# One decoder block on one core: the second feed-forward's seven-product pair over all of K at chunks 7 and 8, and the attention branch in blocks of 512 columns

## The chip, the cores and the metric

The kernel runs on one core of a Trainium2 chip. The metric is the device time of one execution in microseconds. The core's engines run side by side and each takes its instructions in the order in which they are written down for it: TensorE (PE, matrix products into eight accumulator banks of 128 x 512 fp32), VectorE (DVE), ScalarE (ACT), GpSimd (POOL) and SyncE (SP), which issues the DMA transfers here.

## What is computed

One layer on 256 tokens of width 1024 in fp32: a SwiGLU feed-forward of hidden width 2816 at half weight, a mixing layer (attention and gated spatial mixing, merged by gates), a second feed-forward, and a last norm.

```python
def swiglu(x, w_gate, w_up, w_down):
    return (jax.nn.silu(x @ w_gate) * (x @ w_up)) @ w_down
...
h = h + 0.5 * swiglu(rmsnorm(h, ffn1_norm[l]), ffn1_w_gate[l], ffn1_w_up[l], ffn1_w_down[l])
n = rmsnorm(h, mix_norm[l])
...
y_attn = attn @ w_branch_attn[l]
y_gmlp = gm @ w_branch_gmlp[l]
gates = jax.nn.sigmoid(n @ w_gate[l] + b_gate[l])
merged = gates[..., :D] * y_attn + gates[..., D:] * y_gmlp
h = h + merged @ w_out[l]
h = h + 0.5 * swiglu(rmsnorm(h, ffn2_norm[l]), ffn2_w_gate[l], ffn2_w_up[l], ffn2_w_down[l])
return rmsnorm(h, final_norm)
```

## The kernel before

**Products in three matmuls.** Weights come from memory in fp32 and are split into a high part (a cast, on ScalarE) and a low part (a subtraction, on VectorE), in `split` (L255 to L258). A product of two split blocks takes three matmuls: high by high, high by low, low by high (`mm3`, L249 to L253). In the text a product is one such group of three for 128 tokens, 128 rows of K and up to 512 columns.

**Weight units.** All weights stand in one list, `units`, in the order in which TensorE wants them. A unit is a tile w0, w1, ...; it is loaded in two halves of 512 KB (raw, seven buffers), split half by half, and kept in a ring of five tiles (w). `unit(i, ahead)` splits up to `ahead` units past the one that is wanted, so VectorE and ScalarE work some units in front of TensorE.

**Chunks.** A feed-forward's gate and up matrices are cut into 11 chunks (`NC`) of 256 hidden features, each 512 columns: gate, then up. A plain chunk is two units (K in two halves) and 16 products into two banks, one for each half of the tokens (f2_90 and f2_91 are those of chunk 9 of the second feed-forward). Behind a chunk, `Hidden.glu` (L578) makes silu of the gate half on ScalarE (f2s), multiplies it by the up half on VectorE (f2a, two operations) and transposes it (f2t); DMAs carry it to another layout, and it is settled as a split operand (f2h).

**The pair of chunks.** `chunk_pair` (L408) computes two chunks together. `seven` (L378) takes two blocks of K and forms the 2 x 2 by 2 x 2 block product (token halves by chunks) in seven products in place of eight. It needs four combinations of the activations ("forms", made by `make_forms`, L399, on VectorE and split), and four combinations of the weights, which are made on VectorE as well: a "single" unit holds three quarters of the weights as they are, and the "sums" unit after it has four 512-wide additions (L205 to L208) and is then split like any other. Four of the products (p1, p5, p6, p7) go to banks shared by several outputs, the others to the banks acc0_0, acc0_512 and acc1_0. In both feed-forwards the pair is chunks 6 and 7, with `PAIR_K` = 3 sevens for the first six of K's eight blocks, and a rest unit with eight plain products for the last two. A copy of p1 on ScalarE (L421) and additions on VectorE (L422 to L425, L435) combine the banks. In the second feed-forward the units are w78 to w83 (single and sums by turns), w84 (the rest) and w85 for the start of chunk 8.

**Who sets the order.** In the first part of the first feed-forward the order on VectorE and ScalarE is the one written. In the second feed-forward a scheduler places the instructions of each engine when the program is built, and they run in that order. Buffers (the ring, the raws, the banks) are handed on by semaphores: a new user waits for the last reader.

**The merge.** `merge` (L1007) does one half of 512 columns of the two branches at a time; the spatial branch (pg) is 512 columns wide, the attention branch (pa) 256, for each quarter p and each token half j. VectorE multiplies by the gate, adds and transposes (L1023 to L1025), SP writes the quarter to memory (`m_way`) and reads it back in another layout (`from_way`); `settle` splits it into mg, the operand of the output product.

Of the kernel before, what the change touches and what calls it, by code (L numbers as in the profile page):

```python
# [46 lines left out]
PAIR = {"f1": 6, "f2": 6}  # L47
PAIR_K = 3
# [3 lines left out]
def block_kernel(ctx, tc, t, out):  # L52
# [63 lines left out]
    def add_chunks(name):  # L116


        c = PAIR[name]
        first = add_units(name, 2 * c)  # L120
        units.extend((f"{name}s2", i, what) for i in range(PAIR_K) for what in ("single", "sums"))
        units.extend((name, i) for i in range(2 * c, 2 * NC - 3))
        return first
# [173 lines left out]
    def token_factors(name):  # L297
# [15 lines left out]
        return [r[:, j:j + 1] for j in range(NT)]  # L313
# [64 lines left out]
    def seven(name, at, i, tokens_of, acc, shared, forms, last, ahead=DEEP):  # L378
# [18 lines left out]
        product(acc, name, (1, 0), d, of(w, 3), False)  # L397
# [10 lines left out]
    def chunk_pair(name, at, nT, forms, ahead):  # L408
# [7 lines left out]
        for i in range(PAIR_K):  # L416
            seven(name, at + 2 * i, i, tokens_of, acc, shared, forms[i], i == PAIR_K - 1, ahead)
# [9 lines left out]
        def rest(e):  # L427
            w = unit(at + 2 * PAIR_K, ahead)
            for k in range(2):
                for j in range(NT):  # L430
                    product(acc, name, (j, 512 * e), tokens_of(KB - 2 + k, j),
                            tuple(w[:, 2 * e + k, two, :] for two in range(2)), k == 1)
# [8 lines left out]
    def chunk_of(name, first, nT, c, forms):  # L441

        at = c - PAIR[name]
        if at == 0:
            pending[name] = chunk_pair(name + "p", first + 2 * c, nT, forms, DEEP)
        if at in (0, 1):
            return pending[name](at)
        return chunk(first + 3 * (at > 0), nT, name, c, ahead=DEEP)

    def pair_forms(name, tags, block):  # L450

        normed = []
        for n, rows in ((0, 4), (1, 2)):
            normed.append(sump.tile([P, 4, S // 32, 32], F32, tag="sum", name=f"{name}normed{n}"))
            for k in range(rows):
                block(4 * n + k, normed[n][:, k])

        def make():
            to = [act.tile([P, 2 - n, 4, 2, P], F32R, tag=tag, name=f"{name}forms{n}") for n, tag in enumerate(tags)]
            to = [to[0][:, 0], to[0][:, 1], to[1][:, 0]]  # L460
            for i in range(PAIR_K):
                make_forms(lambda j, k: normed[i // 2][:, 2 * (i % 2) + k, 4 * j:4 * j + 4, :], to[i], f"{name}form{i}")
            return to
        return make
# [102 lines left out]
    class Hidden:  # L567
# [10 lines left out]
        def glu(self, c, ps, rs):  # L578
            self.turned[c] = tmp.tile([P, NT, CH], F32, tag="hg", name=f"{self.name}t{c}")
            a = tmp.tile([P, NT, CH], F32, tag="a", name=f"{self.name}a{c}", bufs=1)  # L580
            for j in range(NT):
                sg = tmp.tile([P, CH], F32, tag="s", name=f"{self.name}s{c}{j}")
                nc.scalar.activation(sg, ps[j][:, :CH], AF.Silu, scale=rs[j])  # L583
                nc.vector.scalar_tensor_tensor(a[:, j], ps[j][:, CH:], rs[j], sg, op0=ALU.mult, op1=ALU.mult)
# [102 lines left out]
    with in_order():  # L687
        x = inputs_of(front[:, KB:KB + KB * ROW])
        split_to(f1 + 3)
# [5 lines left out]
        forms_of = pair_forms("f1p", ("nC", "ws"), lambda k, to: nc.scalar.activation(  # L695
            to.rearrange("p q c -> p (q c)"), x[:, k], AF.Identity, scale=front[:, k:k + 1]))
        sum_parts("1")
        sums.append(chunk(f1, nT, "f1", 1))
        rs = token_factors("1")
        sums.append(chunk(f1, nT, "f1", 2))  # L700
# [504 lines left out]
```

## Time and profile before

| what | value |
| --- | --- |
| time, median of 3 runs | 514.98 us (514.45 to 516.18) |
| profiled execution | 514.82 us, of which its span 513.1 us |
| TensorE's granted clock | 1.00 |
| DMA | 126.82 MB, mean 247 GB/s |
| GpSimd busy | 12.0 us |
| ScalarE busy | 299.8 us |

The rows of the profile give a start, a duration, the engine, the line of the kernel and the operation, with out<-in by the program's names. x2 in a row of the timeline stands for two instructions one behind the other, and its duration is for both. Durations of rows that follow each other overlap a little, since an instruction starts before its predecessor has quite ended; what an instruction costs its engine is the distance from its start to the next one's. A bracket at a row's end is idle time of the engine ahead of it, and what ended that.

### The profile page before, as it was taken

The page shows a single profiled execution, that of the slowest core. Times are in us where ns is not written, and L with a number is a line of the kernel's source. Part 1 is how long each engine was busy: PE and PEld are TensorE (multiplying, and loading weights), DVE is VectorE, ACT ScalarE, POOL GpSimd, SP SyncE. Part 2 cuts the span into 40 slices and gives each one's busy share as a digit, 9 for nine tenths or more (in the row PEclk, how much of TensorE's full clock was granted, in tenths as well). Part 3 has the DMA queues.
Part 4 walks back from the last instruction along what each step waited for, and adds up shares of the span by engine and source line. Part 5 has one row for each costly group of instructions (what it writes and reads, how often), then busy time and mean ns, then how long its engine had stood idle before and what let it go on. Part 6 is the DMA issues. An engine that isn't in the chain of part 4 may idle for free.

```text
span 513.1 us, 6849 instructions
## 1 busy us (share of the span) xinstructions
PE 505.6 (99%) x2359; PEld 421.3 (82%) x2359; DVE 442.9 (86%) x645; ACT 299.8 (58%) x427; POOL 12.0 (2%) x25
## 2 busy tenths in 40 slices
PE   8999999999999999999999999999999999999995
PEld 6888888888888888888888898888888888888884
DVE  6897999999997956589976776997979999999964
ACT  7984549546573736667465603767725756566702
POOL 0010000000000010000000000001000000000002
PEclk9999999999999999999999999999999999999999
DMA  8998587798765886796899664928799558999302
GB/s 316 374 327 335 138 294 255 256 310 278 232 211 201 282 310 206 194 335 240 205 375 309 247 192 142 319 91 270 249 275 295 203 160 259 349 351 283 136 0 82
DMA packets 63922, 126.82 MB, mean 247 GB/s; under 512 B 11664, under 2 KB 36752, under 8 KB 63760
## 3 DMA queue, kind: packets, MB, share of 16 engines
q1 hardware_dynamic: 63600, 126.06, 74.6%
q8 instruction: 18, 0.29, 0.2%
q10 hardware_dynamic: 288, 0.33, 0.2%
q14 instruction: 16, 0.13, 0.1%
HBM read 113.26 MB, written 13.11 MB: 246 GB/s over the span
## 4 chain that ended last, share of the span: by engine, by line
PE 97%; DMA 1%; DVE 0%; issue 0%; ACT 0%; POOLq 0%; DVEq 0%; POOL 0%; ACTq 0%
PE f L253 12%; PE f L252 12%; PE f L251 12%; PE accdown L253 4%; PE accdown L251 4%; PE accdown L252 4%; PE acch L253 4%; PE acch L252 4%; PE acch L251 4%; PE acc L225 3%; PE g L252 3%; PE g L253 3%; PE g L251 3%; PE acc L230 1%; PE accf2p L253 1%; PE accf2p L252 1%
## 5 line engine op out<-in xcount | busy, mean ns | idle before, releaser
L258 DVE TENSOR_TENSOR w<-raw,w 128x1024 fp32r<-128x1024 f32 (+1 forms) x180 | 204.0, 1173 | 15.7 <-ACT w L256 15.6
L256 ACT CAST w<-raw 128x1024 fp32r<-128x1024 f32 (+1 forms) x180 | 173.8, 1015 | 24.4 <-PE f L253 7.9
L253 PE MATMUL f<-w,n 128*128 128x512 f32 x272 | 105.8, 389 | 0.0
L251 PE MATMUL f<-w,n 128*128 128x512 f32 x272 | 105.8, 389 | 0.0
L252 PE MATMUL f<-w,n 128*128 128x512 f32 x272 | 105.8, 389 | 0.0
L252 PEld LDWEIGHTS f<-w,n 128*128 128x128 f32 x272 | 51.1, 188 | 10.6
L251 PEld LDWEIGHTS f<-w,n 128*128 128x128 f32 x272 | 51.1, 188 | 10.6
L253 PEld LDWEIGHTS f<-w,n 128*128 128x128 f32 x272 | 51.1, 188 | 10.6
L256 ACT CAST w<-sum 128x1024 fp32r<-128x1024 f32 x28 | 29.5, 1053 | 31.7 <-DVE sum L206 21.5
L258 DVE TENSOR_TENSOR w<-sum,w 128x1024 fp32r<-128x1024 f32 x28 | 33.8, 1218 | 0.5 <-ACT w L256 0.5
L251 PE MATMUL accdown<-w,f1h 128*128 128x512 f32 x68 | 26.5, 389 | 0.0
L252 PE MATMUL accdown<-w,f1h 128*128 128x512 f32 x68 | 26.5, 389 | 0.0
L253 PE MATMUL accdown<-w,f1h 128*128 128x512 f32 x68 | 26.5, 389 | 0.0
L251 PE MATMUL g<-w,n 128*128 128x512 f32 x64 | 24.9, 389 | 0.0
L252 PE MATMUL g<-w,n 128*128 128x512 f32 x64 | 24.9, 389 | 0.0
L251 PE MATMUL acch<-w,f2h 128*128 128x512 f32 x64 | 24.9, 389 | 0.0
L252 PE MATMUL acch<-w,f2h 128*128 128x512 f32 x64 | 24.9, 389 | 0.0
L253 PE MATMUL acch<-w,f2h 128*128 128x512 f32 x64 | 24.9, 389 | 0.0
L253 PE MATMUL g<-w,n 128*128 128x512 f32 x64 | 24.9, 389 | 0.0
L225 PE MATMUL acc<-mg,w 128*128 128x512 f32 x64 | 17.0, 393 | 0.0
L583 ACT ACTIVATE f2s<-f,rstd 128x256 f32<-128x256 f32 x18 | 8.1, 473 | 12.5 <-PE f L253 11.4
L256 ACT CAST mg<-mixed 128x256 fp32r<-128x256 f32 x8 | 2.9, 404 | 21.3 <-DMA mixed<-mway 21.3
(279 smaller groups left out, 918.5 us busy)
## 6 DMA issues: line engine op xcount, KB each, us to landing
raw<-in_f SPq DMA_DIRECT2D x72, 512.0 KB, 6.2
raw<-in_f2d SPq DMA_DIRECT2D x22, 512.0 KB, 7.4
raw<-in_gate SPq DMA_DIRECT2D x16, 512.0 KB, 6.3
raw<-in_f1s SPq DMA_DIRECT2D x14, 512.0 KB, 6.6
raw<-in_f1d SPq DMA_DIRECT2D x14, 512.0 KB, 5.2
raw<-in_out SPq DMA_DIRECT2D x8, 512.0 KB, 5.4
raw<-in_f2s SPq DMA_DIRECT2D x6, 512.0 KB, 6.9
f1way<-f1t SPq DMA_DIRECT2D x11, 256.0 KB, 6.5
```

What stands on the lines that cost most here:

```text
L225: nc.tensor.matmul(ps, st, both.rearrange("p two n -> p (two n)"), start=first, stop=last)
L230: nc.tensor.matmul(ps[:, n:], st, both[:, 0, :], start=False, stop=False)
L251: nc.tensor.matmul(ps, sh, mh, start=first, stop=False)
L252: nc.tensor.matmul(ps, sh, ml, start=False, stop=False)
L253: nc.tensor.matmul(ps, sl, mh, start=False, stop=last)
L256: nc.scalar.copy(hi, src)
L258: nc.vector.tensor_sub(lo, src, hi.bitcast(F32))
L583: nc.scalar.activation(sg, ps[j][:, :CH], AF.Silu, scale=rs[j])
```

## The change

1. A table `PAIRS` takes the place of `PAIR` and `PAIR_K`: the first feed-forward keeps chunks 6 and 7 with three sevens, the second has chunks 7 and 8 with four sevens over all of K, hence no rest unit. Its units are now w80 to w87, and w88 starts chunk 9.
2. With four sevens nothing is left for the fourth bank (acc1_512), so the last quarter comes out with its sign turned. It is handed on so, and `glu` multiplies it by the negated norm factor, which `token_factors` now makes as well (one small operation on VectorE behind GpSimd's power).
3. The forms of the second feed-forward's pair are made at chunk 4 for chunk 3, and in other buffers; the reloads of the residual (`ht1`, `ht`) and of the last gain move to other chunks.
4. The attention branch is computed 512 columns at a time. Its product, addition and transpose are 512 wide, one for each token half, and each half of the tokens is written out for both quarters at once, with eight smaller writes in place of four.

```diff
-PAIR = {"f1": 6, "f2": 6}
-PAIR_K = 3
+PAIRS = {"f1": {6: 3}, "f2": {7: 4}}
...
+        minus = small.tile([P, NT], F32, tag="minus", name=f"minus{name}", bufs=1)
+        nc.vector.tensor_scalar(minus, r, -1.0, None, op0=ALU.mult)
...
+        ends = last and whole
         w = unit(at, ahead)
         product(shared, name, (1,), a, of(w, 0), last)
-        product(acc, name, (0, 0), b, of(w, 1), False)
-        product(acc, name, (0, 512), form(3), of(w, 2), False)
+        product(acc, name, (0, 0), b, of(w, 1), ends)
+        product(acc, name, (0, 512), form(3), of(w, 2), ends)
...
-        for i in range(PAIR_K):
-            seven(name, at + 2 * i, i, tokens_of, acc, shared, forms[i], i == PAIR_K - 1, ahead)
+        for i in range(n):
+            seven(name, at + 2 * i, i, tokens_of, acc, shared, forms[i], i == n - 1, ahead, n == 4)
...
         def rest(e):
-            w = unit(at + 2 * PAIR_K, ahead)
-            for k in range(2):
+            for k in range(2 * n, KB):
+                w = unit(at + 2 * n + (e if n == 2 else 0), ahead)
...
-                (nc.vector.tensor_sub if e else nc.vector.tensor_add)(x, acc[j, 512 * e], x)
-            return [to[e][:, j] for j in range(NT)]
+                if (j, 512 * e) in acc:
+                    (nc.vector.tensor_sub if e else nc.vector.tensor_add)(x, acc[j, 512 * e], x)
+            return [to[e][:, j] for j in range(NT)], e and n == 4
...
-            for j in range(NT):
+            for j, (r, minus) in enumerate(zip(rs, negative or rs)):
+                r = minus if j else r
...
-    ht1 = act.tile([P, NT, D], F32, tag="nD", name="ht1")
-    for j in range(NT):
-        nc.sync.dma_start(ht1[:, j, :], t["by_tokens"][j * P:(j + 1) * P, :])
     for c in range(2, NC):
...
+        if c == max(PAIRS["f1"]) + 2:
+            ht1 = act.tile([P, NT, D], F32, tag="nD", name="ht1")
...
-            for p in (2 * hf, 2 * hf + 1):
-                m_turned[p] = tmp.tile([P, NT, UC], F32, tag="hg", name=f"mt{p}")
-                for j in range(NT):
-                    ps = bank(f"pa{p}{j}")[:, :UC]
-                    branch(ps, w, aoT, j, slice((p % 2) * UC, (p % 2 + 1) * UC))
...
-                nc.sync.dma_start(by_token(m_way[p]), m_turned[p])
+            m_turned = tmp.tile([P, NT, 2 * UC], F32, tag="back", name=f"mt{hf}", bufs=1)
+            for j in range(NT):
+                ps = bank(f"pa{hf}{j}")
+                branch(ps, w, aoT, j, slice(2 * UC))
...
+                for p in range(2):
+                    nc.sync.dma_start(by_token(m_way[2 * hf + p])[:, j], m_turned[:, j, p * UC:(p + 1) * UC])
...
-        if c == 3:
+        if c == 4:
             forms = forms_of()
...
-        elif c == PAIR["f2"] + 3:
+        elif c == 7:
             gain4 = act.tile([P, D], F32, tag="ws", name="gain4")
```

The order of instructions changes around the pair of the second feed-forward. First TensorE, at the end of the last seven. Before (accf2p1_0 is the bank acc1_0, w84 the rest unit, whose 24 matmuls begin here):

```order
L252 MATMUL accf2p6_3665<-w83_3642,f2pforms1_3401 128x512
L253 MATMUL accf2p6_3665<-w83_3642,f2pforms1_3401 128x512
L251 MATMUL accf2p1_0_3669<-w83_3642,n31_2827 128x512
L252 MATMUL accf2p1_0_3669<-w83_3642,n31_2827 128x512
L253 MATMUL accf2p1_0_3669<-w83_3642,n31_2827 128x512
L251 MATMUL accf2p0_0_3634<-w84_3673,n31_2827 128x512
L252 MATMUL accf2p0_0_3634<-w84_3673,n31_2827 128x512
L253 MATMUL accf2p0_0_3634<-w84_3673,n31_2827 128x512
```

After (w87 is the fourth seven's sums unit, f2_90 and f2_91 the banks of chunk 9):

```order
L255 MATMUL accf2p71_0_3703<-w87_3725,n31_2767 128x512
L256 MATMUL accf2p71_0_3703<-w87_3725,n31_2767 128x512
L257 MATMUL accf2p71_0_3703<-w87_3725,n31_2767 128x512
L255 MATMUL f2_90_3874<-w88_3752,n30_2766 128x512
L256 MATMUL f2_90_3874<-w88_3752,n30_2766 128x512
L257 MATMUL f2_90_3874<-w88_3752,n30_2766 128x512
L255 MATMUL f2_91_3875<-w88_3752,n30_2766 128x512
L256 MATMUL f2_91_3875<-w88_3752,n30_2766 128x512
L257 MATMUL f2_91_3875<-w88_3752,n30_2766 128x512
```

The last seven is now followed at once by chunk 9. The bank of f2_91 is the one that held p1; its first matmul waits for the copy of p1 on ScalarE.

Next VectorE, around the gated product of chunk 5 (f2a5). Before (sum81 to sum83 are weight sums, f2t5 the transposed product):

```order
L258 TENSOR_TENSOR w81_3566<-sum81_0_3567,w81_3566 128x2x512
L258 TENSOR_TENSOR w81_3566<-sum81_1_3568,w81_3566 128x2x512
L584 SCALAR_TENSOR_TENSOR f2a5_3613<-f2_50_3533,rstd3_3177,f2s50_3614 128x256
L584 SCALAR_TENSOR_TENSOR f2a5_3613<-f2_51_3534,rstd3_3177,f2s51_3617 128x256
L205 TENSOR_TENSOR sum83_0_3643<-raw82_0_3450 128x512
L258 TENSOR_TENSOR w82_3621<-raw82_0_3450,w82_3621 128x512
L206 TENSOR_TENSOR sum83_0_3643<-raw82_0_3450,raw82_1_3485 128x512
L207 TENSOR_TENSOR sum83_1_3644<-sum83_0_3643,raw82_1_3485 128x512
L585 STREAM_TRANSPOSE f2t5_3612<-f2a5_3613 128x512
L258 TENSOR_TENSOR w82_3621<-raw82_1_3485,w82_3621 128x2x512
L208 TENSOR_TENSOR sum83_1_3644<-sum83_1_3644,raw82_1_3485 128x512
L258 TENSOR_TENSOR w83_3642<-sum83_0_3643,w83_3642 128x2x512
```

After (f2pform2 and f2pform3 are forms of the pair's last two sevens):

```order
L262 TENSOR_TENSOR w81_3515<-sum81_0_3516,w81_3515 128x2x512
L598 SCALAR_TENSOR_TENSOR f2a5_3560<-f2_50_3482,rstd3_3117,f2s50_3561 128x256
L598 SCALAR_TENSOR_TENSOR f2a5_3560<-f2_51_3483,rstd3_3117,f2s51_3564 128x256
L262 TENSOR_TENSOR f2pforms2_3447<-f2pform2_3448,f2pforms2_3447 128x4x128
L409 TENSOR_TENSOR f2pform3_3455<-f2normed4_3267 128x128
L410 TENSOR_TENSOR f2pform3_3455<-f2normed4_3267 128x128
L411 SCALAR_TENSOR_TENSOR f2pform3_3455<-f2pform3_3455,f2normed4_3267 128x128
L412 TENSOR_TENSOR f2pform3_3455<-f2pform3_3455,f2normed4_3267 128x128
L262 TENSOR_TENSOR w82_3570<-raw82_0_3375,w82_3570 128x512
L211 TENSOR_TENSOR sum81_1_3517<-sum81_0_3516,raw80_1_3320 128x512
L262 TENSOR_TENSOR f2pforms2_3447<-f2pform3_3455,f2pforms2_3447 128x4x128
L212 TENSOR_TENSOR sum81_1_3517<-sum81_1_3517,raw80_1_3320 128x512
```

Before, TensorE begins the pair right behind chunk 5, and the units of the first two sevens (w78 to w81) were split ahead of f2a5. Now chunk 6 lies between chunk 5 and the pair, and ahead of f2a5 there are w80 and only the first half of w81; the rest of w81 and w82 to w87 stand behind it.

Last ScalarE, around the copy of p1. Before:

```order
L256 CAST w83_3642<-sum83_0_3643 128x2x512
L256 CAST w84_3673<-raw84_0_3540 128x2x512
L256 CAST w83_3642<-sum83_1_3644 128x2x512
L256 CAST w84_3673<-raw84_1_3575 128x2x512
L256 CAST w85_3691<-raw85_0_3579 128x2x512
L421 COPY f2p0_3751<-accf2p1_3630 128x512
L256 CAST f2h_3058<-f2back1_3607 128x8x4x32
L583 ACTIVATE f2s60_3791<-f2p0_3751,rstd3_3177 128x256
L256 CAST w85_3691<-raw85_1_3624 128x2x512
```

After:

```order
L260 CAST w87_3725<-sum87_0_3726 128x2x512
L260 CAST w88_3752<-raw88_0_3662 128x2x512
L260 CAST w87_3725<-sum87_1_3727 128x2x512
L260 CAST w88_3752<-raw88_1_3685 128x2x512
L260 CAST w89_3770<-raw89_0_3689 128x2x512
L260 CAST w89_3770<-raw89_1_3710 128x2x512
L260 CAST w90_3789<-raw90_0_3714 128x2x512
L260 CAST w90_3789<-raw90_1_3734 128x2x512
L260 CAST w91_3805<-raw91_0_3738 128x2x512
L260 CAST w91_3805<-raw91_1_3755 128x2x512
L428 COPY f2p70_3826<-accf2p71_3664 128x512
L260 CAST w92_3876<-raw92_0_3759 128x512
```

Before, the copy stood ahead of the second half of w85 (chunk 8). Now it stands behind the splits of all of chunks 9 and 10 (w88 to w91).

More of the change, by code (lines that the diff above doesn't have):

```diff
@@ L116, in add_chunks @@
     def add_chunks(name):
[L119 to L123, printed above, removed]
+        at, plain, c = {}, 0, 0
+        while c < NC:
+            at[c] = len(units)
+            n = PAIRS[name].get(c, 0)
+            units.extend((f"{name}p{c}", i, what) for i in range(n) for what in ("single", "sums"))
+            more = 4 - n if n else 2
+            units.extend((name, plain + i) for i in range(more))
+            plain += more
+            c += 2 if n else 1
+        return at
     f1 = add_chunks("f1")
@@ L376, in product, with seven @@
         mm3(banks[key], st, w, first, last)
-    def seven(name, at, i, tokens_of, acc, shared, forms, last, ahead=DEEP):
+    def seven(name, at, i, tokens_of, acc, shared, forms, last, ahead=DEEP, whole=False):
         a, b, d = tokens_of(2 * i, 0), tokens_of(2 * i + 1, 0), tokens_of(2 * i + 1, 1)
@@ L396, in seven @@
         product(shared, name, (6,), form(2), of(w, 2), last)
-        product(acc, name, (1, 0), d, of(w, 3), False)
+        product(acc, name, (1, 0), d, of(w, 3), ends)
     def make_forms(of, to, name):
@@ L406, in make_forms, with chunk_pair @@
         split(to[:, :, 0, :], to[:, :, 1, :], f)
-    def chunk_pair(name, at, nT, forms, ahead):
+    def chunk_pair(name, at, nT, n, forms, ahead):
         acc, shared = {}, {}
@@ L441, in chunk_of @@
     def chunk_of(name, first, nT, c, forms):
[L443 to L448, printed above, removed]
+        n = PAIRS[name].get(c)
+        if n:
+            pending[name, c + 1] = chunk_pair(f"{name}p{c}", first[c], nT, n, forms, DEEP)
+            return pending[name, c + 1](0)
+        if (name, c) in pending:
+            return pending.pop((name, c))(1)
+        return chunk(first[c] - 2 * c, nT, name, c, ahead=DEEP), False
     def pair_forms(name, tags, block):
         normed = []
[L453 to L456, printed above, removed]
-        def make():
[L459 to L462, printed above, removed]
+        most = max(PAIRS[name].values())
+        for k in range(2 * most):
+            if k % 4 == 0:
+                normed.append(sump.tile([P, 4, S // 32, 32], F32, tag="sum", name=f"{name}normed{k}"))
+            block(k, normed[-1][:, k % 4])
+        def make():
+            to = []
+            for i in range(most):
+                if i % 2 == 0:
+                    two = act.tile([P, min(2, most - i), 4, 2, P], F32R, tag=tags[i // 2], name=f"{name}pforms{i}")
+                to.append(two[:, i % 2])
+                make_forms(lambda j, k: normed[i // 2][:, 2 * (i % 2) + k, 4 * j:4 * j + 4, :], to[i], f"{name}pform{i}")
             return to
@@ L1063, in block_kernel @@
         hidden.move(c)
-        hidden.glu(c, ps, rs)
+        hidden.glu(c, ps, rs, negative and minus)
         if c == 3:
@@ L1155, in chunks, with plain_units @@
         return w.reshape(2, 4, P, -1, 512).transpose(3, 0, 2, 1, 4).reshape(-1, P, 4, 512)
-    def paired(units, c):
-        last = np.concatenate([units[2 * c + 1][:, 2:], units[2 * c + 3][:, 2:]], 1)
-        return np.concatenate([units[:2 * c], last[None], units[2 * c + 4:]])
+    def plain_units(name, whole):
+        got, c = [], 0
+        while c < NC:
+            n = PAIRS[name].get(c, 0)
+            if n == 0:
+                got += [whole[2 * c], whole[2 * c + 1]]
+            elif n == 2:
+                got += [whole[2 * c + 1], whole[2 * c + 3]]
+            elif n == 3:
+                got.append(np.concatenate([whole[2 * c + 1][:, 2:], whole[2 * c + 3][:, 2:]], 1))
+            c += 2 if n else 1
+        return np.stack(got)
     turned = np.arange(D).reshape(4, 2, 4, P // 4).transpose(1, 0, 2, 3).reshape(-1)
```

54 lines of the change are left out of this document (28 added, 26 removed).

## The prediction

> **What bounds the kernel now.** I read the page first (busy shares, then the chain that ended last), then the table of waits of TensorE, then the windows around the changed places, then the rows of VectorE and ScalarE there.
>
> ```profile
> PE 505.6 (99%) x2359; PEld 421.3 (82%) x2359; DVE 442.9 (86%) x645; ACT 299.8 (58%) x427; POOL 12.0 (2%) x25
> PE 97%; DMA 1%; DVE 0%; issue 0%; ACT 0%; POOLq 0%; DVEq 0%; POOL 0%; ACTq 0%
> ```
> ```profile
> engine line waited for: us in total, times, longest us
> PE warm L103 <- DVE zeros L100: 1.2, 1, 1.2
> PE f L681 <- ACT n L657: 0.2, 1, 0.2
> ```
> ```profile
> core 0: us, PE busy (x) PEld busy (x) DVE busy (x) ACT busy (x) POOL busy (x), PEclk, DMA share, GB/s
> 400.00:450.00 50.00, 50.00 (x222) 41.42 (x221) 49.19 (x69) 29.80 (x39) 0.00 (x0) 1.00 0.76 242
> ```
> TensorE waits 1.4 us in the whole run, and 97% of the chain is its own work: the time is a count of matmuls. In the stretch that the change rebuilds, though, VectorE is busy for 49.19 of 50 us. So every matmul saved counts only while VectorE, which halves and sums the weights, stays ahead.
>
> **The change part by part: matmuls.**
> ```profile
> 396.99 0.39 PE L253 MATMUL f<-w,n 128*128 128x512 f32 x1
> 397.21 0.39 PE L251 MATMUL accf2p<-w,n 128*128 128x512 f32 x1
> ...
> 411.49 0.39 PE L251 MATMUL accf2p<-w,n 128*128 128x512 f32 x1
> ```
> ```profile
> L251 PE MATMUL accf2p<-w,n 128*128 128x512 f32 x17 | 6.6, 389 | 0.0
> ...
> L251 PE MATMUL accf2p<-w,f2pforms 128*128 128x512 f32 x12 | 4.7, 389 | 0.0
> ```
> The printed 389 ns overlap; issue is what counts. Three sevens (21 products of 3 matmuls) run from 397.21 to 411.49: 4.76 us a seven, 0.68 a product, 0.227 a matmul. The pair has 17 + 12 = 29 products; after the change four sevens make 28. **Saved: 3 x 0.227 = 0.68 us.**
>
> ```profile
> core 0: us, PE busy (x), PEclk, DMA share, GB/s
> 292.39:298.14 5.75, 5.75 (x48) 1.00 0.72 224
> 303.61:309.36 5.75, 5.75 (x48) 1.00 0.73 203
> ```
> The attention branch's 48 matmuls of 256 columns take 5.75 us a half (0.120 each); 24 of 512 at 0.227 take 5.45. **Saved: 2 x 0.30 = 0.60 us.** The Trainium skill ("TensorE: Matmul & The Clock Gate", section "Wait — 56ns, not 53.3ns?") speaks against this part: it puts the fixed cost of a matmul at some 2.5 ns beside N columns at 2.4 GHz. An estimate by it is 48 x 109.2 = 5.24 us against 24 x 215.8 = 5.18, so 0.06 a half, and the sum would be 0.48 us later. The trace's 120 and 227 ns are both above these figures, with a larger part that does not scale; I keep the rows.
>
> The branch also feeds a transfer for which TensorE could wait:
> ```profile
> 308.45 0.42 DVE L1023 TENSOR_TENSOR mixed<-pa,mixed 128x256 f32<-128x256 f32 x1
> ...
> 313.11 0.45 DVE L1025 STREAM_TRANSPOSE mt<-mixed 128x256 f32<-128x256 f32 x1
> ```
> ```profile
> 311.08 2.88 SPq L1026 DMA_DIRECT2D mway<-mt  x2
> 314.05 5.30 SPq L557 DMA_DIRECT2D mixed<-mway  x8
> ```
> ```profile
> 318.79 0.71 ACT L256 CAST mg<-mixed 128x256 fp32r<-128x256 f32 x2 [8.85 <-DMA mixed<-mway]
> ```
> ```profile
> 320.53 1.78 PE L225 MATMUL acc<-mg,w 128*128 128x512 f32 x7
> ```
> Twelve 256-wide operations from 308.45 to 313.56 become six of 512, about 1 us sooner in all, but quarter 2 now leaves complete only with the second token half. Its write went at 311.08 and its read-back at 314.05; the write would now go at about 312.5, the read-back at 314.1 to 314.7, with eight writes issued for four. The cast ends at 319.50, TensorE takes it at 320.53, and will ask 0.60 sooner: 0.4 us remain. Bounds 0 to 0.7 of stall; I take 0, since arrival hardly moves.
>
> **The pair, VectorE.** Prices are start-to-start, rows being back to back:
> ```profile
> 394.54 0.69 DVE L205 TENSOR_TENSOR sum<-raw 128x512 f32<-128x512 f32 x1
> 395.14 0.69 DVE L206 TENSOR_TENSOR sum<-raw,raw 128x512 f32<-128x512 f32 x1
> ...
> 399.41 0.87 DVE L584 SCALAR_TENSOR_TENSOR f2a<-f,rstd,f2s 128x256 f32<-128x256 f32 x2
> 400.20 0.68 DVE L205 TENSOR_TENSOR sum<-raw 128x512 f32<-128x512 f32 x1
> ...
> 402.60 0.70 DVE L585 STREAM_TRANSPOSE f2t<-f2a 128x512 f32<-128x512 f32 x1
> 403.23 1.18 DVE L258 TENSOR_TENSOR w<-raw,w 128x1024 fp32r<-128x1024 f32 x1
> ...
> 406.07 1.22 DVE L258 TENSOR_TENSOR w<-raw,w 128x1024 fp32r<-128x1024 f32 x1
> 407.21 1.22 DVE L258 TENSOR_TENSOR w<-sum,w 128x1024 fp32r<-128x1024 f32 x1
> ...
> 415.02 0.28 DVE L402 TENSOR_TENSOR f2form<-f2back 128x128 f32<-128x128 f32 x1
> 415.22 0.29 DVE L403 TENSOR_TENSOR f2form<-f2back 128x128 f32<-128x128 f32 x1
> ```
> So 0.60 us for a 512-wide operation, 1.14 for a 1024-wide one (split or settling), 0.20 for a 128-wide form, 0.63 for a transpose, 0.39 for a gated product. A seven costs VectorE 0.60 + 1.14 + 4 x 0.60 + 2 x 1.14 = 6.4 us against 4.76 on TensorE; a plain unit 2.27 against 5.44. Four sevens for three sevens and the rest unit add 6.4 - 2.3, a form (1.4), and drop one 512-wide subtraction: about +4.9 us of VectorE.
>
> An idle stretch ahead could pay for that, but the order does not let it. In the new order the gated products of chunk 5 (f2a5) stand ahead of the rest of the first seven's sums (w81) and of everything for w82 to w87. They need TensorE's end of chunk 5 (396.99 + 0.39 = 397.38 by the rows above; before and after alike, in the time of before) and ScalarE's half-gates:
> ```profile
> 398.14 0.83 ACT L583 ACTIVATE f2s<-f,rstd 128x256 f32<-128x256 f32 x2
> ...
> 406.01 1.99 ACT L256 CAST w<-raw 128x1024 fp32r<-128x1024 f32 x2
> 407.91 0.57 ACT L421 COPY f2p<-accf2p 128x512 f32<-128x512 f32 x1
> ```
> With 0.4 us for the second half-gate, f2a5 cannot end before about 398.3. Behind it the order has, up to the low half of w87's second part, 21 operations of 512 (12.6), 12 of 1024 (13.6), 12 forms (2.4), two transposes (1.3) and two gated products (0.8): 30.7 us, so 429.0; chains with ScalarE can add up to 0.9. TensorE runs chunk 6 (48 x 0.227 = 10.88) from 397.21 and starts the pair at 408.09; it asks for that half after three sevens and five products, 408.09 + 14.28 + 3.40 = 425.8. **Late by 3.2 to 4.2 us**; the first shortage is at w85, whose first half is ready at 420.2 and wanted at 419.6. The pair ends at 430.4 to 431.3 for 427.1.
>
> **The pair, ScalarE and the banks.** Seven of eight accumulator banks belong to the pair. Chunk 9's first bank is free; its second (f2_91, wanted from its fourth matmul, 427.1 + 0.68 = 427.8) is that of product p1, which a copy on ScalarE must clear. Before, that copy ran at 407.91, beside TensorE's third seven, with the rest unit's eight products (5.4 us) still to come. After, it stands behind ten 1024-wide casts: w87, w88, w89, w90, w91, two each. The first of them needs w87's first sum, on VectorE at 398.3 + 26.1 = 424.4. At (407.91 - 406.01) / 2 = 0.95 each that is 433.9, and the copy 0.5 more: 434.4, with the chains up to 435.3; the transfers for w91 wait for buffers that the same late splits free, and may add to that. So TensorE stands from about 431 to 435: **f2_91 starts 6.6 to 7.5 us late. I take 7.2**, which holds the 3 to 4 us above and is not added to them.
>
> **Costed at nothing.**
> ```profile
> 31.83 1.62 POOL L312 TENSOR_TENSOR rstd<-ms,nhalf 128x2 f32<-128x2 f32 x1 [30.10 <-DVE ms L308]
> ```
> ```profile
> 31.66 4.63 DVE L258 TENSOR_TENSOR w<-raw,w 128x1024 fp32r<-128x1024 f32 x4
> ```
> The negated factors are one 128x2 operation that makes VectorE wait for GpSimd's power: up to 1.6 us in f1 and again in f2. In f1 the four halves split right there are units 7 and 8, which TensorE begins at 44.5 and 49.9 (24 matmuls a unit), so some 8 us of stock hide it; without that cover it would cost its 1.6. The first feed-forward's pair keeps its chunk and its three sevens; its forms and the reload of the residual move to another buffer, behind chunk 8 on SP's queue, where it is wanted only at the down product. The moved reloads in f2 are wanted there as well. The chunks behind the pair have 5.44 us of TensorE for each 2.27 of VectorE, and TensorE, being late, only widens that.
>
> **The sum**, against the profiled execution (span 513.1, 514.82 in all, 1.72 outside the span; the median of the runs is 514.98): 513.1 - 0.60 - 0.68 + 7.2 = 519.0, and 520.7 with the 1.72.
>
> **The rivals.**
> 1. *Only the late splits.* If the copy finds ScalarE free sooner (casts of w89 to w91 waiting for nothing that TensorE does, done early), f2_91 waits for the pair alone: 514.82 - 1.28 + 3.2 to 4.2 = 516.7 to 517.7. For it: ScalarE is busy for 29.80 of 50 us. Against: it runs in its written order, and the copy is last.
> 2. *Nothing is late: the other side.* The stock of split weights built in the extra plain chunk carries the pair. The place is VectorE's wait at f2a5, the price is the whole 7.2. It decides if w87's second half is ready 3.2 us sooner than I count and the copy 6.6, that is, if f2a5's wait is not what dates the work behind it. Then 514.82 - 1.28 = 513.5, 0.25% below before, within the 0.3% that a measurement of this kernel can tell from no change. For it, VectorE has idle time ahead, 2.7 of 10 us here:
> ```profile
> 370.00:380.00 10.00, 7.29 (x11) 1.00 0.85 275
> ```
> Against: the order puts the wait behind that idle time.
> 3. *More than I count.* The transfer of the branch (0.7), the late transfers of w91 and a down part that starts with less VectorE time in hand (the 4.9 us put off, 1 to 2 of them felt) come on top: 521.5 to 523.5.
>
> **How the numbers follow.** Forecast 0.58, rival 1 0.15, rival 2 0.12, rival 3 0.15. Predicted 520.7. The forecast's own bounds are 520.1 to 521.0; with rivals 1 and 3 the range is 516.0 to 523.5, which leaves out rival 2. Faster by over 0.3% needs 1.5 us, more than both savings: 0.04. Within 0.3% is rival 2 and half-covered cases: 0.13. Slower 0.83.
>
> **What would show it.** The branch: 48 matmuls of 512 columns, 24 in 5.45 us a half. The pair: 28 products. TensorE idle before w85's and w87's halves, waiting for VectorE's L262, about 3 to 4 us in all; then one wait of about 4 us before chunk 9's second bank, put down to the copy (L428) on ScalarE; VectorE idle before f2a5 for some microseconds. If TensorE shows no idle time between 405 and 440, rival 2 holds and my count of VectorE's rows is wrong; if it waits for splits but not for the copy, rival 1.

## The result, and the profile after

The changed kernel takes 522.58 us (median of 5 runs, 521.04 to 523.02), the kernel before 514.45 on the same chip (514.21 to 516.18). The ratio is **1.0146**, with a 95% interval of 1.0123 to 1.0168: slower by 1.5%. The profiled execution took 521.04 us, of which its span is 519.3; the prediction was 520.7, with a span of 519.0. The median of the runs lies 1.9 us above the prediction.

The page of the changed kernel, with the busy shares of the engines and the chain that ended last:

```profile
PE 505.9 (97%) x2308; PEld 417.6 (80%) x2308; DVE 446.2 (86%) x645; ACT 302.7 (58%) x432; POOL 11.8 (2%) x25
PE 92%; DVE 3%; ACT 2%; issue 1%; DMA 1%; POOLq 0%; DVEq 0%; POOL 0%; ACTq 0%
```

There are 51 matmuls fewer, the 48 of the branch and the 3 of the pair, and yet TensorE's share of the chain has fallen from 97% to 92%. VectorE and ScalarE stand in the chain now. The table of TensorE's waits (total, times, longest) says where:

```profile
PE f L255 <- ACT f2p L428: 3.3, 1, 3.3
PE accf2p L256 <- DVE w L262: 2.3, 3, 0.8
PE warm L102 <- DVE zeros L99: 1.2, 1, 1.2
PE accf2p L255 <- ACT w L260: 0.3, 1, 0.3
```

Beside the warm-up's (L102), which the kernel before has too, these are the two kinds of wait that the prediction named, and no others. TensorE's timeline places them (start, duration; in the bracket the idle time and what ended it):

```profile
418.95 0.49 PE L255 MATMUL accf2p<-w,f2pforms 128*128 128x512 f32 x1 [0.29 <-ACT w L260]
...
420.27 0.50 PE L256 MATMUL accf2p<-w,f2pforms 128*128 128x512 f32 x1 [0.83 <-DVE w L262]
...
426.81 0.50 PE L256 MATMUL accf2p<-w,f2pforms 128*128 128x512 f32 x1 [0.82 <-DVE w L262]
...
429.08 0.50 PE L256 MATMUL accf2p<-w,f2pforms 128*128 128x512 f32 x1 [0.64 <-DVE w L262]
...
434.49 0.50 PE L255 MATMUL f<-w,n 128*128 128x512 f32 x1 [3.29 <-ACT f2p L428]
```

The first four are halves of w85 and w87, the last is f2_91, the bank that held p1. The brackets add up to 5.9 us, but this is less than what was lost. A bracket counts from a matmul's modelled end, 0.39 us after its start, though the next could start after 0.227; and the first matmul behind a wait takes 0.34. Counted start to start, the pair and f2_91's turn together lose 7.84 us.

VectorE's timeline, from chunk 5's gated product (L598) to the first addition of the banks (L429):

```profile
396.08 0.48 DVE L598 SCALAR_TENSOR_TENSOR f2a<-f,rstd,f2s 128x256 f32<-128x256 f32 x1 [2.96 <-ACT f2s L597]
396.76 0.48 DVE L598 SCALAR_TENSOR_TENSOR f2a<-f,rstd,f2s 128x256 f32<-128x256 f32 x1 [0.20 <-ACT f2s L597]
...
427.81 1.22 DVE L262 TENSOR_TENSOR w<-sum,w 128x1024 fp32r<-128x1024 f32 x1
428.94 8.03 DVE L262 TENSOR_TENSOR w<-raw,w 128x1024 fp32r<-128x1024 f32 x7
436.89 0.68 DVE L429 TENSOR_TENSOR f2p<-accf2p,f2p 128x512 f32<-128x512 f32 x1
```

It idles ahead of f2a5, then runs, with one marked pause of 0.19 us at 411.05, to the low half of w87's second part, which ends at 429.03 (427.81 + 1.22); TensorE takes that at 429.08. And ScalarE, with the ten casts and the copy behind them:

```profile
424.38 1.05 ACT L260 CAST w<-sum 128x1024 fp32r<-128x1024 f32 x1 [3.07 <-DVE sum L210]
425.34 1.04 ACT L260 CAST w<-raw 128x1024 fp32r<-128x1024 f32 x1
426.28 1.04 ACT L260 CAST w<-sum 128x1024 fp32r<-128x1024 f32 x1
427.23 6.73 ACT L260 CAST w<-raw 128x1024 fp32r<-128x1024 f32 x7
433.86 0.58 ACT L428 COPY f2p<-accf2p 128x512 f32<-128x512 f32 x1
```

The first cast waits for w87's first sum, as forecast. The copy ends at 434.44 (433.86 + 0.58), and f2_91 starts at 434.49.

The branch, in windows of one half of 512 columns each (length, TensorE busy and instructions, clock, DMA share, GB/s):

```profile
291.91:297.35 5.44, 5.44 (x26) 1.00 0.68 224
302.79:308.23 5.44, 5.44 (x26) 1.00 0.66 164
```

5.44 us for 5.75 (the count takes in two matmuls at the edges).

So the ledger of the profiled execution is: start-up 0.48 us shorter, branch 0.65, pair 0.68, stalls +7.84, small gaps of the matmuls right behind the waits +0.2; together +6.2, and the span went from 513.1 to 519.3. The start-up is not the change's doing: the code there is the same, and e1, below, whose start-up is that of the kernel before, is 0.30 us shorter there as well.

### The profile page after: what moved, and what is told of

It is laid out like the page before. It is cut to its first block, busy times and chain, and to the rows that moved or that the text cites. A ratio compares the mean times of both kernels' runs of the same rounds, so it can differ in the third digit from the quotient of the medians.

```text
span 519.3 us, 6754 instructions
## 1 busy us (share of the span) xinstructions
PE 505.9 (97%) x2308; PEld 417.6 (80%) x2308; DVE 446.2 (86%) x645; ACT 302.7 (58%) x432; POOL 11.8 (2%) x25
## 4 chain that ended last, share of the span: by engine, by line
PE 92%; DVE 3%; ACT 2%; issue 1%; DMA 1%; POOLq 0%; DVEq 0%; POOL 0%; ACTq 0%
PE f L255 12%; PE f L257 12%; PE f L256 12%; PE accdown L256 4%; PE accdown L255 4%; PE accdown L257 4%; PE acch L257 3%; PE acch L255 3%; PE acch L256 3%; PE acc L229 3%; PE g L256 3%; PE g L257 3%; PE g L255 3%; ACT w L260 2%; PE acc L234 1%; PE accf1p L256 1%
## 5 line engine op out<-in xcount | busy, mean ns | idle before, releaser
L262 DVE TENSOR_TENSOR w<-raw,w 128x1024 fp32r<-128x1024 f32 (+1 forms) x180 | 203.0, 1170 | 12.8 <-ACT w L260 12.7
L260 ACT CAST w<-raw 128x1024 fp32r<-128x1024 f32 (+1 forms) x180 | 173.6, 1012 | 28.0 <-PE f L257 12.3
L260 ACT CAST w<-sum 128x1024 fp32r<-128x1024 f32 x30 | 31.4, 1050 | 27.9 <-DVE sum L210 19.1
L262 DVE TENSOR_TENSOR w<-sum,w 128x1024 fp32r<-128x1024 f32 x30 | 36.7, 1228 | 2.8 <-ACT w L260 2.5
L597 ACT ACTIVATE f1s<-f,rstd 128x256 f32<-128x256 f32 x18 | 8.2, 472 | 13.2 <-PE f L257 11.6
```

What stands on the lines that cost most here:

```text
L260: nc.scalar.copy(hi, src)
L262: nc.vector.tensor_sub(lo, src, hi.bitcast(F32))
L597: nc.scalar.activation(sg, ps[j][:, :CH], AF.Silu, scale=r)
```

## The experiments

The mechanism was seen; what was open is whether its parts can be taken away one by one, that is, whether the late splits and the late copy are separate costs, or whether VectorE's lack of time comes back elsewhere. In the diffs, `behind(key)` is a small addition: what is issued in its block is placed behind the named instructions in the order of its engine. It adds lines, so L262, L428 and L598 of the changed kernel have higher numbers in the kernels that use it. The diffs show the main cut of each edit; `...` stands for the rest of it. f2[7] is the number of the pair's first unit, w80, and f2d has the down product's units: f2d[0] is w92, f2d[1] w94.

| kernel | what differs | median us | ratio to before (95%) |
| --- | --- | --- | --- |
| e1 | before, with the branch of the change | 514.66 | 0.9995 (0.9986 to 1.0004) |
| e2 | changed, copy of p1 early | 526.82 | 1.0231 (1.0217 to 1.0245) |
| e3 | changed, f2a5 behind w81 | 523.34 | 1.0165 (1.0151 to 1.0179) |
| e4 | e2 and e3 | 527.52 | 1.0246 (1.0232 to 1.0260) |
| e5 | changed, a form and a settling later | 521.74 | 1.0133 (1.0120 to 1.0146) |
| e6 | e2, w92 behind chunk 7's half-gates | 523.06 | 1.0148 (1.0134 to 1.0163) |
| e7 | e5 and e6 | 523.52 | 1.0167 (1.0154 to 1.0180) |
| e8 | changed, three sevens at chunk 7 | 515.84 | 1.0019 (1.0010 to 1.0027) |
| e9 | e7, f2a10 ahead of w94 and w95 | 521.18 | 1.0110 (1.0085 to 1.0134) |
| e10 | changed, four sevens at chunk 6 | 529.84 | 1.0276 (1.0248 to 1.0304) |
| e11 | e8, f2a10 ahead of w93 and w94 | 515.42 | 1.0007 (0.9997 to 1.0016) |
| e12 | e9 less eight additions | 516.68 | 1.0036 (1.0022 to 1.0051) |

### e1: the branch alone

The kernel before with part 4 of the change, whose diff is shown above.

> The kernel before with part 4 of the change alone (attention branch 512 columns wide). Theory A (rows of before): 24 matmuls at 0.227 us for 48 at 0.120 save 0.30 us a half, nothing waits: 0.65 us below before, about 513.8 for 514.45. Rival R (fixed cost of a matmul is only 2.5 ns): 0.1 us, which can't be told from nothing. Rival S: the transfer of the merged quarters arrives later than TensorE wants it, 0 to 0.7 us back, a wait of TensorE for mg would show.

The time cannot be told from no change. Yet TensorE passes the branch 0.66 us sooner in e1's trace, as the prediction has it. About 0.5 us was lost ahead of it, 0.3 of it in a wait of the mixing part at 229.6 that is 0 to 0.8 us long in the kernels' traces, though their code is the same there; and 0.2 us of the gain was lost again behind it. In two other kernels with this branch, the read-back did cost something; e9's timeline at the output product:

```profile
321.55 3.94 PE L236 MATMUL acc<-mg,w 128*128 128x512 f32 x16 [0.75 <-DVE mg L277]
```

e5 has 0.93 us there, and the changed kernel's own profile none. So the saving is 0.6 us of matmuls, and the read-back takes part of it, or all, in some executions.

### e2: the copy ahead of w89 to w91

```diff
-            seven(name, at + 2 * i, i, tokens_of, acc, shared, forms[i], i == n - 1, ahead, n == 4)
+            seven(name, at + 2 * i, i, tokens_of, acc, shared, forms[i], i == n - 1, 1 if n == 4 and i == 3 else ahead, n == 4)
```

> The changed kernel with the copy of p1 six casts earlier on ScalarE (the last seven splits one unit ahead in place of four, so that the copy stands behind w89 and not behind w91). Theory A (bank held by a late copy): the 3.3 us wait before chunk 9's second bank goes, the four short waits at w85 to w87 stay: 3.3 to 3.6 us below the changed kernel, about 519.0 for 522.6, and the profile's wait for the copy is below 0.3 us. Rival B (late weights alone date everything): within 0.5 us of the changed kernel, the wait moves to the splits of w89 or w90.

The wait for the copy went, and the time rose by 4 us. Two new waits appear, on VectorE and, through it, on TensorE. The rows of VectorE and ScalarE, and the line of TensorE's table:

```profile
440.79 0.48 DVE L598 SCALAR_TENSOR_TENSOR f2a<-f2p,rstd,f2s 128x256 f32<-128x256 f32 x1 [3.36 <-ACT f2s L597]
```
```profile
439.30 1.05 ACT L260 CAST w<-raw 128x1024 fp32r<-128x1024 f32 x1 [1.90 <-DMA raw<-in_f2d]
```
```profile
PE acch L255 <- DVE f2a L598: 4.3, 1, 4.3
```

In the new order ScalarE has a cast of w92 ahead of the half-gates of chunk 7, and that cast waits for a transfer; VectorE stands behind the half-gates. What VectorE loses there comes out 20 us later at the down product: its banks acch1_0 and acch1_512 are those of chunk 10, which f2a10 must have read. With the pair one chunk later, only chunks 9 and 10 lie between it and the down product. In the changed kernel it does not show, because TensorE has been made 8 us late already: f2a10 ends at 459.05 there, and TensorE takes the bank at 459.81. So neither theory of the expectation gave the time. The wait of 4.3 us is longer than the 3.3 that it replaced, and behind it TensorE ran at half clock for 6.8 us, which the last section takes up.

### e3 and e4: chunk 5's gated product out of the way

```diff
+        if c == 6:
+            with behind((f2[7] + 1, 1)):
+                hidden.glu(5, held, rs)
...
```

The rest keeps chunk 5's banks until then and puts the first half of w82 behind w81's second half as well.

> The changed kernel with chunk 5's gated products, and the first half of w82, put behind the whole split of w81 on VectorE and ScalarE; the copy stays late. Theory A (the wait for chunk 5 dates VectorE's row): VectorE gets some 3.2 us back, the split waits fall from 2.6 us recorded to under 1, and the copy comes 3 us sooner, so its wait stays near 3 us (it follows w87's sums): about 519.5 for 522.6. Rival B (the ring: w82 can't be split before TensorE leaves w77 at 396.2, so VectorE only waits elsewhere): within 0.7 us of the changed kernel.

The rival was right in kind. VectorE no longer waits for f2a5 and gets some 3.6 us ahead (w83's first sum starts at 402.00, in the changed kernel at 405.62), and loses nearly as much at the next obstacle (VectorE's and ScalarE's timelines):

```profile
409.83 1.23 DVE L273 TENSOR_TENSOR w<-sum,w 128x1024 fp32r<-128x1024 f32 x1 [3.42 <-ACT w L271]
```
```profile
407.87 0.62 ACT L271 CAST w<-raw 128x512 fp32r<-128x512 f32 x1 [3.44 <-PE f L260]
```

The cast is the first of w84. It needs the ring tile of w79, which TensorE reads to the end of chunk 6 (matmuls of L260). With five tiles VectorE cannot be further ahead than that, wherever f2a5 stands. The time, 523.34, is 0.8 us above the changed kernel's; the clock was halved behind the copy's wait in the profiled run, the longest of the five (524.49).

> The edits of the two runs before together. Theory A: both waits add up, so about 6.5 us below the changed kernel, 515.5 to 516.3 for 522.6, with one or two split waits of under 1 us left at w85 and w87. Rival B: no better than the early copy alone (519.0).

e4 has both edits, and e2's wait of 4.3 us with them: 527.52. Neither theory gave that: the gains do not add up as A had it, and the rival's 519.0 was the forecast for e2, which took 526.82.

### e5: work of VectorE moved out of the pair

The forms and the settling of chunks 2 and 3, some 3 us on VectorE, go behind w87.

```diff
-        hidden.form_behind(c, ("h", "nB"))
-        hidden.move(c)
+        if c == 6:
+            hidden.leave(5)
+        else:
+            if c == 7:
+                with behind((f2[7] + 7, 1)):
+                    hidden.form_behind(6, ("h", "nB"))
+                    hidden.settle(1)
+            hidden.form_behind(c, ("h", "nB"))
+            hidden.move(c)
...
```

> The changed kernel with one block of VectorE's work (the form and the settling of chunks 2 and 3 for the down product, some 3.1 us with its split) moved from the middle of the pair to behind w87, where the kernel before has it, behind the pair. Theory A, as the gate run has mended it: from the moment TensorE leaves w79 the ring lets VectorE go on, and it then has 20.3 us of work up to w87's second half for 17.7 us of TensorE. With 3.1 us less the waits at w85 to w87 go (below 0.6 us recorded, for 2.6). The copy still stands behind w91 and comes 3 us sooner, against a pair that ends 4 us sooner: its wait grows to 4 to 5 us, and the halved clock behind it costs some 2.8: about 521.3, 0 to 2 us below the changed kernel. Rival (the fourth seven is too much wherever the rest stands): split waits stay near 2.6 us.

The split waits fell from 2.6 us to 1.3, the copy's wait stayed at 3.28, and behind it the clock was halved in the profiled run (as in the last section below). The time is as expected, 521.74, but the steps are not: the split waits should have fallen below 0.6 and the copy's wait risen to 4 to 5 us. The profiled run is the longest of the four (523.12) and has the read-back's 0.93 us in it.

### e6 and e7: both waits of the pair treated

e6 is e2 with w92's split behind chunk 7's half-gates on ScalarE, so that e2's new wait can't arise. e7 has e5's edit too.

```diff
-            return quarters(i, hf)
+            with behind("silu") if i == f2d[0] and "silu" in order else ExitStack():
+                got = quarters(i, hf)
...
```

> The early copy again, with the splits of w92 put behind the two half-gates of chunk 7 on ScalarE, so that these don't stand behind a transfer. Theory A (the early copy was right, its loss came from VectorE's 3.4 us of idle time behind those half-gates): no wait for the copy, none at chunk 10 and none of 4.3 us at the down product; the waits at w85 to w87 stay: 518.0 to 518.8. Rival (any shift of the order at this place ends in a late bank): a wait of 3 us or more at the down product stays, 522 or more.

> The edits of the two runs beside it together: form and settling behind w87, copy behind w89, half-gates of chunk 7 ahead of w92. Theory A: no wait of TensorE over 0.6 us is left in the second feed-forward and the saved matmuls show: 513.8 to 514.8 for 515.1 before. Rival (VectorE's 4.9 us more must come back somewhere, at the latest in the down product): waits of 2 us or more there, 516 to 519.

At the pair both did what they should: e7's pair is late by 1.84 us, where the changed kernel's is late by 7.84. Neither gained in time. In e6's profiled run, the shortest of its four (521.28), TensorE still waits 2.4 us for f2a10, where e2 has 4.3, and no halved clock follows; the median, 523.06, is in the rival's range. e7's 523.52 is above both ranges of its expectation. In e7 the wait has moved to the down product (waits of TensorE, then VectorE's timeline there):

```profile
PE acch L258 <- DVE f2a L609: 4.3, 1, 4.3
PE accf2p L259 <- DVE w L273: 1.2, 2, 0.6
```
```profile
454.13 0.70 DVE L610 STREAM_TRANSPOSE f2t<-f2a 128x512 f32<-128x512 f32 x1
454.76 4.05 DVE L273 TENSOR_TENSOR w<-raw,w 128x1024 fp32r<-128x1024 f32 x4
458.74 0.86 DVE L609 SCALAR_TENSOR_TENSOR f2a<-f,rstd,f2s 128x256 f32<-128x256 f32 x2
```

VectorE has no gap at all here; it is simply behind. f2a10 (458.74) stands behind four halves of w94 and w95, though its half-gates were ready at 456.1. So the rival that VectorE's work must come back is right in kind, though its range had no halved clock behind that wait, which is some 2.8 us of the 4.5 by which it was too low. A part of the price is again a matter of place in the row.

### e8: only the place

```diff
-PAIRS = {"f1": {6: 3}, "f2": {7: 4}}
+PAIRS = {"f1": {6: 3}, "f2": {7: 3}}
```

> The changed kernel with three sevens and a rest unit in the second feed-forward, but at chunks 7 and 8 as after the change. It tells the fourth seven from the place. Theory A (the fourth seven and the missing rest unit make the waits): no waits at the pair, 514.0 to 515.2. Rival (the place one chunk later is at fault: less room behind it): waits as in the changed kernel, 518 or more.

Nothing waits at the pair. One wait is left, at the same bank as in e2:

```profile
PE acch L255 <- DVE f2a L598: 1.1, 1, 1.1
```

515.84, 0.6 us above theory A's range: by the ratios of e8 and e1, the place by itself costs 1.2 us. The rest, at this place, comes with the fourth seven.

### e9: the gated product of chunk 10 first

```diff
-        return split(w[:, sl, 0, :], w[:, sl, 1, :], raws.pop((i, hf)), later)
+        with behind("gated") if i == f2d[1] and "gated" in order else ExitStack():
+            return split(w[:, sl, 0, :], w[:, sl, 1, :], raws.pop((i, hf)), later)
...
```

The rest keeps `unit` from splitting w94 and w95 before chunk 10's products are placed.

> The kernel of e7 (forms late, copy early) with one more move: the gated product of chunk 10 (f2a10) and its half-gates stand ahead of the splits of w94 and w95 on VectorE and ScalarE. In e7 TensorE waited 4.3 us at 459.26 for f2a10, which stood behind four halves of w94 and w95, and then ran for some 6 us at half clock (about 2.8 us). Theory A, it is the position in VectorE's row: the wait falls to 1.5 us or less, no half clock behind it, no new wait for w94 or w95 above 0.5, time 516.8 to 518.2. Rival, it is VectorE's amount of work: the wait moves on to w94 to w96 (2 to 3 us for the splits), time 519.5 to 522.

Both theories have a share. The wait for f2a10 fell from 4.3 to 0.9 us and no halved clock followed, which was the place in the row. But waits for splits in the down product took over, as the rival said, the longest at 468.10 and the last at 480.19 (TensorE's waits; those of accf2p are the pair's, which e7 has too):

```profile
PE acch L263 <- DVE w L277: 1.7, 3, 1.2
PE accf2p L263 <- DVE w L277: 1.2, 2, 0.6
...
PE acch L262 <- DVE f2a L613: 0.9, 1, 0.9
```

The time is in the rival's range: 521.18. VectorE (the third of the busy times) is full from 405 on:

```profile
405.00:482.00 77.00, 73.08 (x314) 57.86 (x313) 76.59 (x107) 46.20 (x58) 0.00 (x0) 1.00 0.80 255
```

### e12: less work for VectorE

The edit is in the branch of `quarters` for the sums units, on top of e9. It leaves out the sums of w83 and w85, so that the second and third sevens compute other products: a kernel for measuring only.

```diff
+        elif i in (f2[7] + 3, f2[7] + 5):
+            r = raws.pop((i - 1, hf)).rearrange("p one (n c) -> p (one n) c", c=512)
+            to = w[:, 2 * hf:2 * hf + 2]
...
```

> The kernel of e9 (521.18) with eight 512-wide additions of VectorE left out: the sums units w83 and w85 are split from the loads of w82 and w84 as they are, so the second and third sevens compute other products; everything else, its order, casts, matmuls and transfers, stays. It takes 8 x 0.60 = 4.8 us of VectorE's work out, about what the fourth seven had added (4.9). In e9 TensorE stood about 5.7 us in all between 420 and 481 in seven short waits for VectorE. Theory A, what is left there is VectorE's amount of work: these waits shrink to 1.5 us in all or less, time 514.0 to 516.3. Rival, the ring of five tiles and the transfers set the dates and VectorE will only idle: 3 us or more of the waits stay, time 518 to 521.

The pair's waits are gone, and of the 6.3 us that e9 loses start to start between 420 and 481, 2.7 are left, all in the down product. So 3.6 us of stalls went with 4.8 us of VectorE's work. The time went from 521.18 to 516.68, by 4.5 us, or by 3.8 as a share of the kernel before (ratios 1.0110 and 1.0036). Of the 5.5 us between the two profiled executions 1.9 lie in the start-up, the mixing part and the read-back, which the edit does not touch. The time is 0.4 us above theory A's range, and its 1.5 us of waits were too few; but most of what e9 lost is VectorE's amount of work, about three quarters of a microsecond for each that was taken away, and the rival's 3 us of waits and 518 us are out. One thing the edit can't keep apart: the casts of w83 and w85 no longer wait for sums of VectorE either, so a hand-over between the engines went with the work.

VectorE is no less full than in e9:

```profile
405.00:482.00 77.00, 75.34 (x330) 61.25 (x329) 76.90 (x105) 48.95 (x62) 0.00 (x0) 1.00 0.88 275
```

In the same 77 us it has got further, and so has TensorE (330 matmuls for 314). So a full engine by itself does not show that the others wait for it; the waits and this experiment do.

### e10: only the fourth seven

```diff
-PAIRS = {"f1": {6: 3}, "f2": {7: 4}}
+PAIRS = {"f1": {6: 3}, "f2": {6: 4}}
```

The forms are made at chunk 3 again, which is the rest of the edit.

> The changed kernel with the four sevens at chunk 6, the old place: the fourth seven alone. ScalarE's order again has the copy of p1 behind ten casts, those of the last sums unit and of both chunks that follow. Theory A, the fourth seven makes the stall wherever the pair stands: VectorE has two sevens (12.8) and 4.3 us of forms, transposes and settling behind chunk 5's gated product (ends at 400.2), so the last half is ready at about 417 against 414.9, and the copy at about 422.7 against 416.9; one wait of 3 us or more for the copy, time 518.5 to 522. Rival, the place makes it: with the pair one chunk further from the down product nothing is late, time 513.5 to 515.5.

Theory A's direction, and twice its size: 529.84, where 522 was the upper end. The copy's wait is there (3.2 us), but the larger part lies ahead of it. VectorE's timeline at chunk 5's gated product:

```profile
388.57 1.18 DVE L262 TENSOR_TENSOR w<-raw,w 128x1024 fp32r<-128x1024 f32 x1
396.97 0.48 DVE L598 SCALAR_TENSOR_TENSOR f2a<-f,rstd,f2s 128x256 f32<-128x256 f32 x1 [7.21 <-ACT f2s L597]
```

I had taken the order of before, in which w81 was split ahead of f2a5. In e10's order the rest of w79's sums stands behind f2a5, and VectorE idles for 7.21 us with work at hand. TensorE, which begins the pair at once behind chunk 5, then waits 2.1 us already at w79 and 2.4 at w83. Behind those two the clock is halved for 3.4 us in the profiled run, the shortest of the four (528.03). Against e10, the plain chunk that the change puts between f2a5 and the pair is worth about 7 us to the changed kernel, the halved clock included. So the place costs 1.2 us with three sevens and gains 7 with four.

### e11: the better order for three sevens

e8 with e9's edit, for w93 and w94.

> Three sevens at chunk 7 (as e8, 515.84 with one wait of 1.1 us for the gated product of chunk 10), and that gated product ahead of the splits of w93 and w94. Theory A, the position of the product is all that the place costs: the wait is below 0.3 and the time 514.3 to 515.0, as the branch alone (514.66) or better. Rival, the later pair leaves VectorE short in the down product whatever the order: the wait goes to the splits of w93 to w95, time 515.5 to 516.5.

The wait for f2a10 is gone, and 0.6 us for a split took its place, as the rival said. The time is 515.42, between the two ranges, 0.4 us under e8's and no different from before. With fewer sevens VectorE's lack is small, and so is what the order can bring. No version ran that beats the kernel before.

## Why the prediction came out as it did

**Right: the mechanism.** The order on VectorE behind f2a5, the late halves of w85 and w87, the copy of p1 behind ten casts: all three stand in the profile as described, and the lost time is theirs. Rivals 1 and 2 are out, since TensorE waits for the copy as well.

**Right in size: the matmuls.** Branch 0.65 us for 0.60, pair 0.68 by 51 matmuls fewer. By the estimate from the Trainium skill ("TensorE: Matmul & The Clock Gate", "Wait — 56ns, not 53.3ns?") the branch would have saved 0.06 a half; the measured 5.44 for 5.75 speaks for the row.

**A little short: the dates.** All dates of the pair fall 1.16 us sooner in the changed kernel (start-up 0.48, branch and what follows it 0.68). So measured, w87's second half was forecast for 427.8 to 428.7 and ended at 429.03; the copy for 433.2 to 434.1 and ended at 434.44. Both are 0.3 us past the upper end. From f2a5 to the end of that half VectorE's 49 operations took 31.7 us for the 30.7 counted; of the 1.0 us of small gaps the trace marks one, 0.19 us behind ScalarE, and the prediction had allowed 0.9 for chains between the engines. f2a5 itself was 0.1 later than forecast. That makes f2_91 late by 7.84 us where 7.2 stood in the sum (6.6 to 7.5). The late splits make 4.4 of them, for 3.2 to 4.2. The shorter start-up nearly made up for it, hence a span of 519.3 for 519.0. That the profiled run meets the sum to 0.3 us is in part luck: the stalls were 0.64 us more than taken, and the 0.48 us of start-up stand in no term of the sum.

**Right: the costs set to nothing.** In the profiled run TensorE waits nowhere else, for the negated factors neither. Only the branch's read-back, taken as 0 with a bound of 0.7, was seen above its bound in other kernels (0.75 and 0.93 us).

**Not foreseen: the runs above the profiled one.** The profiled run is the shortest of the five; the other four took 522.42 to 523.02, 1.4 to 2.0 us more. So the median, 522.58, lies past the forecast's own bounds of 520.1 to 521.0 and in the range only where rival 3 stood (521.5 to 523.5), while none of rival 3's three causes shows in the profiled run. Two things that would do it were seen in other kernels' profiles: the read-back's wait, and a halved clock behind the copy's wait (below). Three of the four have a mean granted clock of 0.993 to 0.995, where the profiled run has 0.999 and the kernel before never had less than 0.996; the fourth has 0.998. By estimate, half clock for 6.8 us in 520 lowers the mean by 0.007. Which it was in each run stays open, as there is a trace of the profiled one only.

**Where the reasoning was too simple: what else a removed wait meets.** The prediction treated f2a5 as what dates VectorE's work, and the copy's place as a cost that could be absent by itself (rival 1, 516.7 to 517.7). The experiments show a chain of limits close behind one another: f2a5, then the ring tile of w79 (e3), then the banks of chunk 10 at the down product (e2, e7). What stands behind most of them, by e12, is VectorE's time. Its busy time (third of the busy times) from 390 to 400, before and after:

```profile
390.00:400.00 10.00, 10.00 (x46) 8.28 (x45) 9.96 (x16) 5.42 (x8) 0.00 (x0) 1.00 0.95 319
```
```profile
390.00:400.00 10.00, 10.00 (x46) 8.29 (x45) 4.86 (x10) 3.99 (x7) 0.00 (x0) 1.00 0.53 199
400.00:482.00 82.00, 76.03 (x328) 60.90 (x327) 81.56 (x117) 48.44 (x61) 0.00 (x0) 1.00 0.78 239
```

It stands 5.1 us longer there than before, has by the prediction's count 4.9 us more to do, and is full for the 82 us that follow. Against that come what stock of split weights there is and 1.3 us of matmuls. So a wait that was taken away at the pair came back at the down product, and most of it went only with the work itself (e12). The prediction's "1 to 2 of 4.9 us felt" in the down part is not seen in the changed kernel, where TensorE's own lateness covers it, but its mechanism is what e7 and e9 ran into.

## What to carry to other kernels

A product that saves matmuls by sums of weights is paid for on the engine that makes the sums; ask whether that engine has idle time between the point where it can't run further ahead (a bank, a ring tile, a wait in its own row) and the point where its work is wanted, and count its work in that stretch before the matmuls saved. When a wait is removed there and the work stays, look for the next bank that the engine hands over: here the time came back there. A full row alone proves nothing: e12's VectorE is as full as e9's. And a copy that clears a bank for the next product belongs ahead of the splits of work that is wanted later, which helps only as far as the first point holds.

## What the runs showed of the hardware

**A wait of some 3.3 us can halve TensorE's clock.** Windows of e3 around f2_91, behind a wait of 3.31 us for the copy that began at 431.95 (length, TensorE busy, clock, DMA share, GB/s), and of the changed kernel, where the wait was 3.29:

```profile
430.81:434.22 3.41, 1.14 (x5) 1.00 0.67 232
434.22:441.05 6.83, 5.80 (x14) 0.50 0.92 306
```
```profile
433.00:435.00 2.00, 0.51 (x2) 1.00 0.96 272
435.00:437.00 2.00, 2.00 (x10) 1.00 0.78 166
```

In e3 the clock is 0.50 for 6.8 us, 5.8 of them behind the wait, and 14 matmuls go at 0.43 us in place of 0.227: 2.8 us more for the same wait. e5 (3.28 us) shows it too, e10 behind its copy's wait of 3.22 does not; the three waits of 4.3 us (e2, e4, e7) all do. e7's matmuls behind its wait:

```profile
459.26 0.79 PE L258 MATMUL acch<-w,f2h 128*128 128x512 f32 x1 [4.26 <-DVE f2a L609]
459.85 0.63 PE L259 MATMUL acch<-w,f2h 128*128 128x512 f32 x1
460.28 0.63 PE L260 MATMUL acch<-w,f2h 128*128 128x512 f32 x1
```

The Trainium skill ("TensorE: Matmul & The Clock Gate", Part 1, "The HAM clock gate") has a free-running window of 3413 ns and half the clock after one idle window. The lengths fit the window: the clock stays at 0.50 for 6.83 us in e2, e3, e4, e5 and e7, and for 3.41 in e10. That the whole window must be idle does not fit: in e3, e4 and e5 the clock fell 2.2 to 2.3 us after TensorE's last matmul had ended. In e10 it fell at 405.08, behind waits of 2.11 and 0.77 us with a single matmul between them; in the 3.41 us ahead of that TensorE was busy for 1.71:

```profile
401.67:405.08 3.41, 1.71 (x6) 1.00 0.00 0
405.08:408.49 3.41, 3.41 (x9) 0.50 0.91 231
```

What decides whether a wait of 3.2 to 3.3 us is followed by half clock stays open.
